# Two-layer diffusion backbone: the low parts of the first layer's up weights made by accumulating DMAs, where VectorE subtracted

## The chip, the cores and the metric

One core of one Trainium2 chip runs the whole program. The metric is device microseconds of one execution. The kernel before took 2854.1 us (median of 3 runs, 2854.01 to 2860.25). The engines are called as in the profile: PE is TensorE (PEld its weight loads), DVE is VectorE, ACT is ScalarE, POOL is GpSimd, SP is SyncE, which issues all DMAs of the kernel before.

## The reference

One inference step through two trunk layers, for 128 context tokens and 512 latent tokens of width 1024, all in float32. A layer is: modulated RMS norm, one input projection, grouped-query attention beside a bidirectional state-space scan, a gated merge with an output projection, and a convolutional feed-forward part. Only this last part is touched:

```
h = modulate(x, sh2, sc2)                                  # RMS norm, scale and shift from w_mod
u = dw_conv(h @ w_up, ffn_conv_w, ffn_conv_b)              # w_up: 1024 x 5632, conv of width 3 over tokens
u_val, u_gate = split(u)                                   # 2816 features each
x = x + g2 * ((silu(u_gate) * u_val) @ w_down)             # w_down: 2816 x 1024
```

The modulation rows (shift, scale, gate of both norms) of a layer are SiLU(cond) @ w_mod + b_mod, for two conditions.

## The kernel before, in words

**Split products.** Weights and activations are float32, the products run on float32r operands. Every operand is split in a high part (rounded to float32r by a cast) and a low part (what the rounding left, again float32r). A product is three matrix products: high by high, high by low, low by high. So each tile of weights needs a high tile and a low tile in SBUF. `wprep` (line 468) makes them: `wraw` loads a raw tile of 128 x 2048 float32, 1 MB, by one DMA on SP; ScalarE casts it into the high tile; VectorE subtracts the high tile from the raw tile into the low tile. The raw tiles (tag wr) have 2 buffers, the high tiles (wh) 3, the low tiles (wl) 3, used in turn by all weights of the kernel.

**Order of the feed-forward part.** The 22 blocks of 128 features (NFF) are taken in three groups, of 8, 8 and 6 blocks. A group is a run of up items (4, 4 and 3 of them) and then two down items. An up item (`up_item`) takes two blocks j and j + 1 of the value half and the same two of the gate half: two weight tiles of 1024 x 256, one of each half. It runs eight half products (`feat_half`): for each block, the value tile's and then the gate tile's, each over 386 and then 256 token columns, with 24 matrix products to a half (8 row blocks of the weights by three). In the first item of the layer the halves come in another order: all four of 386 columns first, then the four of 256. ScalarE takes each half out of PSUM twice (once scaled by the middle tap with the bias, once plain) into buffers whose two edge columns POOL has set to zero, VectorE adds the two other taps, ScalarE and VectorE make the SiLU product, and a split writes the result. In each half product the third matrix product is the first that reads the low tile: the order is high by high, high by low, low by high for each row block.

**Order of weights.** The main loop takes the items in order. Before it records an item it prepares weights up to two tiles beyond what the item itself needs (AHEAD = 2). With three buffers a tile's high and low buffers are those of the tile three places before.

**Beside the first layer's feed-forward part** the modulation rows of the second layer are computed (`mod_item`, class m, the lowest rank on VectorE and ScalarE): VectorE multiplies 8 pieces of w_mod of 256 KB, each by the two conditions, and accumulates them; four short products on TensorE with `pick` sum over the partitions.

**Order on the engines.** All operations are recorded first (class `Flow`), with a cost for each (`_cost`), and a planner (`issue`) simulates the engines' queues in order of time: an operation is placed when its inputs are ready and its buffers free, by rank of class and then order of record. The instructions are issued in the order of planned start times, so each engine's queue is in order, and a waiting instruction holds up what stands behind it. In `_cost` an operation on POOL counts 160 ns, or more for a power. All instructions of the kernel have line 178, that of `record`, so the profile is read by engine, operation and tile.

The lines the change touches: `_cost` (line 183 on), `wprep` (468), a new function `wsum` behind it, and the loop over up items (1491 to 1497).

Of the kernel before, what the change touches and what calls it, by code (L numbers as in the profile page):

```python
# [7 lines left out]
F32 = mybir.dt.float32  # L8
F32R = mybir.dt.float32r
# [3 lines left out]
ALU = mybir.AluOpType  # L13
# [5 lines left out]
P = 128  # L19
# [13 lines left out]
NFF = 22  # L33
# [46 lines left out]
class Flow:  # L80
# [99 lines left out]
    @staticmethod  # L180
    def _cost(lane, fn, outs, ins, kw):
        def free(ap):
            n = 1
            for d in ap.shape[1:]:
                n *= d
            return n

        n = free(outs[0])
        if lane == "dma":
            return free(outs[0]) * outs[0].shape[0] * 4 / 360.0  # L190
        if lane == "pe":
            if fn == "transpose":
                return 110.0
            if ins[0].dtype == F32R:
                return max(n, 256) / 2.4 + 2 if n > 128 else 213.0
            return max(4 * n / 2.4, 213.0)
        psum = any(a.space == PSUM for a in ins)
        scalars = sum(isinstance(a, bass.AP) for k, a in kw.items() if k in ("scale", "bias", "accum_out"))
        if lane == "act":
            return (52 if psum else 95) + 0.832 * n + 93 * scalars  # L200
        if lane == "pool":
            return 165.0 * n + 300 if ALU.pow in kw.values() else 160.0
        scalars = len(ins) - (2 if fn in ("scalar_tensor_tensor", "tensor_tensor") else 1)
        if fn == "tensor_reduce":
            return 70 + 1.04 * free(ins[0])
        if fn == "reciprocal":
            return 70 + 6.2 * n
        if fn in ("tensor_scalar", "tensor_copy", "memset"):
            return 66 + (1.04 if psum else 0.53) * n + 60 * scalars
        if fn == "scalar_tensor_tensor":  # L210
            return 70 + 1.04 * n + 60 * scalars
        return 70 + 1.04 * n
# [129 lines left out]
def hybrid_step_kernel(  # L342
# [5 lines left out]
    flow = Flow(nc)  # L348
    act, dve, pe, pool, dma = flow.act, flow.dve, flow.pe, flow.pool, flow.dma

    kp = ctx.enter_context(tc.tile_pool(name="kp", bufs=1))
    wp = ctx.enter_context(tc.tile_pool(name="wp", bufs=3))
# [11 lines left out]
    def nm(s):  # L364
        uid[0] += 1
        return f"{s}_{uid[0]}"
# [4 lines left out]
    def slabd(shape, dt=F32):  # L371
        return flow.tile(slabs, shape, dt, "slabd", nm("slab"), NSLABD)
# [5 lines left out]
    def t2(shape=(P, 512), dt=F32):  # L378
        return cv(shape, dt)
# [79 lines left out]
    def wraw(parts, wide):  # L459
        r = slabd([P, 2048]) if wide else flow.tile(wp, [P, 2048], F32, "wr", nm("wr"), 2)  # L460
        o = 0
        for ap in parts:
            a, b = ap.shape[1], ap.shape[2]
            dma.dma_start(r[:, o:o + a * b].rearrange("p (a b) -> p a b", a=a), ap)
            o += a * b
        return r, o

    def wprep(parts, wide=False):
        parts, scales = parts if isinstance(parts, tuple) else (parts, None)
        r, n = wraw(parts, wide) if wide != 2 else (None, 2048)  # L470
        hi = flow.tile(wp, [P, 2048], F32R, "wh", nm("wh"), 3)
        lo = flow.tile(wp, [P, 2048], F32R, "wl", nm("wl"), 3)
        if wide == 2:
            for j in range(4):
                o = slice(j * 512, j * 512 + 512)
                flow.cls = "d"
                t = t2()
                flow.cls = "f"
                dma.dma_start(t, parts[0][:, j, :])
                act.copy(hi[:, o], t)  # L480
                dve.tensor_sub(lo[:, o], t, hi[:, o].bitcast(F32))
        elif scales is None:
            act.copy(hi[:, 0:n], r[:, 0:n])
            dve.tensor_sub(lo[:, 0:n], r[:, 0:n], hi[:, 0:n].bitcast(F32))
        else:
            for j, w in enumerate(scales()):
                o = slice(j * 512, j * 512 + 512)
                act.mul(hi[:, o], r[:, o], w)
                dve.scalar_tensor_tensor(lo[:, o], r[:, o], w, hi[:, o].bitcast(F32), ALU.mult, ALU.subtract)
        return hi, lo  # L490

    def w_feat(w, l, c0, n=256, k0=0, kn=8):
        return [w[l, k0 * P:(k0 + kn) * P, c0:c0 + n].rearrange("(k p) f -> p k f", p=P)]
# [4 lines left out]
    def split(hi, lo, src):  # L498
        act.copy(hi, src)
        dve.tensor_sub(lo, src, hi.bitcast(F32))  # L500
# [47 lines left out]
    def feat_half(unit, cw, o, hT, b):  # L548
        ps = psf()[:, 0:HALF[b]]
        uh, ul = unit  # L550
        for kt in range(8):
            wh = uh[:, kt * cw + o:kt * cw + o + P]
            wl = ul[:, kt * cw + o:kt * cw + o + P]
            xh, xl = hT[0][b][:, kt, :], hT[1][b][:, kt, :]
            mm(ps, wh, xh, kt == 0, False)
            mm(ps, wh, xl, False, False)
            mm(ps, wl, xh, False, kt == 7)
        return ps
# [146 lines left out]
    def conv_bufs():  # L705
        raw, cc = cv()[:, 0:COLS + 2], cv()[:, 0:COLS]
        pool.memset(raw[:, 0:1], 0.0)
        pool.memset(raw[:, COLS + 1:COLS + 2], 0.0)
        return raw, cc

    def conv_in(raw, cc, ps, h, w1, b):
        o = HOFF[h]
        act.activation(cc[:, o:o + HALF[h]], ps, AF.Identity, scale=w1, bias=b)
        act.copy(raw[:, 1 + o:1 + o + HALF[h]], ps)

    def conv_taps(raw, cc, w0, w2):
        dve.scalar_tensor_tensor(cc, raw[:, 0:COLS], w0, cc, ALU.mult, ALU.add)
        dve.scalar_tensor_tensor(cc, raw[:, 2:2 + COLS], w2, cc, ALU.mult, ALU.add)

    def silu2(raw, cc):  # L720
        raw = raw[:, 0:COLS]
        act.activation(raw, cc, AF.Tanh)
        dve.scalar_tensor_tensor(cc, raw, 1.0, cc, ALU.add, ALU.mult)
# [19 lines left out]
    def add(specs, fn):  # L743
        items.append((specs, fn))
# [55 lines left out]
    def layer(l):  # L800
# [529 lines left out]
        def up_item(p, jl):  # L1330
            j0 = 8 * p + jl

            def fn(ws):
                if jl == 0:
                    nq = 2 if 8 * p + 4 < NFF else 1
                    S["g", p] = [[slabd([P, 4, PADW], F32R) for _ in range(nq)] for _ in range(2)]
                gs = S["g", p]
                f = S["fw"]
                bufs = {}

                def half(a, s, h):
                    j = j0 + a
                    if h == 0:
                        bufs[a, s] = conv_bufs()
                    raw, cc = bufs[a, s]
                    ps = feat_half(ws[s], 256, a * P, S["h2"], h)
                    conv_in(raw, cc, ps, h, f[:, 1, s, j:j + 1], f[:, 3, s, j:j + 1])
                    if h == 1:
                        conv_taps(raw, cc, f[:, 0, s, j:j + 1], f[:, 2, s, j:j + 1])
                    if h == 1 and s == 1:  # L1350
                        k = jl + a
                        cu = bufs[a, 0][1]
                        silu2(raw, cc)
                        dve.tensor_mul(cc, cc, cu)
                        split(gs[0][k // 4][:, k % 4, 0:COLS], gs[1][k // 4][:, k % 4, 0:COLS], cc)

                if p == 0 and jl == 0:
                    seq = [(a, s, h) for h in range(2) for a in range(2) for s in range(2)]
                else:
                    seq = [(a, s, h) for a in range(2) for s in range(2) for h in range(2)]  # L1360
                for a, s, h in seq:
                    half(a, s, h)
            return fn
# [127 lines left out]
        for p in range(3):  # L1491
            nk = min(8, NFF - 8 * p)
            for jl in range(0, nk, 2):
                j = 8 * p + jl
                add([w_feat(w_up, l, P * j, 256), w_feat(w_up, l, P * (NFF + j), 256)], up_item(p, jl))
                mods_next(mi)
                mi += 1
            if p == 2:
                mods_next(mi)
                if l + 1 < DEPTH:  # L1500
                    add([], lambda _: (small_tables(l + 1, Ss[l + 1]), rope_tables(l + 1, Ss[l + 1])))
            for n in range(2):
                specs = [w_tok(w_down, l, 512 * n, 8 * p + k, min(4, nk - k)) for k in range(0, nk, 4)]
                add(specs, down_item(p, n))
                if p < 2:
                    mods_next(mi)
                    mi += 1
# [4 lines left out]
    for l in range(DEPTH):  # L1512
        layer(l)
# [71 lines left out]
```

## Time and profile before

| what | before |
|---|---|
| median of 3 runs | 2854.1 us |
| the profiled execution's own time | 2856.14 us |
| its span | 2854.3 us |
| granted TensorE clock | 0.998 of full speed |
| TensorE busy | 2816.9 us, 99% |
| VectorE busy | 2067.6 us, 72% |
| ScalarE busy | 1291.3 us, 45% |
| POOL busy | 90.3 us, 3% |
| moved by DMA | 478.45 MB, 168 GB/s in the mean |

The span is the time from the first to the last instruction. The first layer's feed-forward part lies between about 950 and 1420 us of the span (the first load of an up tile is issued at 924.06), the second layer's at its end. In rows that list instructions, a merged line stands for several in a row (x4), the time behind it is from the first start to the last end, and "idle before <-releaser" tells how long the engine had waited for what. In rows of windows the busy columns are PE, PEld, DVE, ACT and POOL, in this order. A matrix product's duration in the profile is longer than the distance to the next one, since they are pipelined.

### The profile page before, as it was taken

Reading aid. Unit: us, or ns where it says so; the run is one execution under the profiler, and the core shown is the slowest. Engines: PE = TensorE matmul, PEld = TensorE weight load, DVE = VectorE, ACT = ScalarE, POOL = GpSimd, SP = SyncE. Lnnn points to the kernel's source line nnn. Section 1 sums busy time; section 2 is a strip of 40 time slices with the busy share of each in tenths; the row PEclk is TensorE's granted clock in tenths of the full one; section 3 lists DMA queues with packets and bytes.
Section 4 is the critical chain, followed back from the end, with each engine's and each line's share of the span. In section 5 each row is a group of like instructions: output and inputs, shape, how many; then the busy total and the mean of one; then the engine's idle time right before and its main releaser. Section 6 shows DMA issues by size and latency. Waiting matters only on the chain.

```text
span 2854.3 us, 41196 instructions
## 1 busy us (share of the span) xinstructions
PE 2816.9 (99%) x15620; PEld 2455.4 (86%) x15620; DVE 2067.6 (72%) x2851; ACT 1291.3 (45%) x2255; POOL 90.3 (3%) x408
## 2 busy tenths in 40 slices
PE   7999999999999999999999999999999999999999
PEld 4898997788788898998979989878887888989898
DVE  7878775987799599997677666598778456545554
ACT  6454544445353453442444645544454325524342
POOL 1100000000000000000011000000000000000000
PEclk9999999999999999999999999999999999999999
DMA  7344344676768546455352323457667654251523
GB/s 260 104 126 137 114 151 155 209 255 245 276 214 277 177 139 213 164 180 174 104 164 83 95 94 100 151 203 251 221 241 250 205 171 136 86 166 65 157 83 111
DMA packets 309679, 478.45 MB, mean 168 GB/s; under 512 B 19808, under 2 KB 139792, under 8 KB 304360
## 3 DMA queue, kind: packets, MB, share of 16 engines
q1 hardware_dynamic: 309480, 475.81, 49.8%
q8 instruction: 123, 2.02, 0.3%
q14 instruction: 76, 0.62, 0.1%
HBM read 384.08 MB, written 91.65 MB: 167 GB/s over the span
## 4 chain that ended last, share of the span: by engine, by line
PE 94%; DMA 3%; DVE 1%; ACT 1%; issue 0%; SPq 0%; DVEq 0%; ACTq 0%
PE pf L178 79%; PE p L178 10%; PE pp L178 3%; PE pq L178 1%; DMA slab<-in_w_mod_dram 0%; DVE tmp L178 0%; DVE wl L178 0%; DMA tmp<-in_state_ssd_dram 0%; DMA tmp<-sz 0%; DMA mw<-in_w_mod_dram 0%; DMA tmp<-in_x_prompt_dram 0%; DVE slab L178 0%; DMA tmp<-xs 0%; ACT tmp L178 0%; DMA slab<-row 0%
## 5 line engine op out<-in xcount | busy, mean ns | idle before, releaser
L178 PE MATMUL pf<-wh,slab 128*128 128x512 f32 x3920 | 1268.9, 400 | 6.5 <-DVE tmp L178 2.5
L178 PE MATMUL pf<-slab,wh 128*128 128x256 f32 (+1 forms) x4416 | 979.5, 311 | 3.3 <-DVE slab L178 1.9
L178 PEld LDWEIGHTS pf<-wh,slab 128*128 128x128 f32 x3920 | 733.3, 189 | 175.8 <-issue 7.6
L178 PE MATMUL pf<-wl,slab 128*128 128x512 f32 x1960 | 781.5, 399 | 0.2 <-DVE wl L178 0.2
L178 PEld LDWEIGHTS pf<-slab,wh 128*128 128x128 f32 x4416 | 741.1, 188 | 11.9 <-issue 5.5
L178 PE MATMUL pf<-slab,wl 128*128 128x256 f32 (+1 forms) x2208 | 684.5, 310 | 0.0
L178 DVE TENSOR_TENSOR wl<-wr,wh 128x2048 fp32r<-128x2048 f32 (+1 forms) x156 | 350.7, 2248 | 144.4 <-ACT wh L178 143.8
L178 PEld LDWEIGHTS pf<-wl,slab 128*128 128x128 f32 x1960 | 369.6, 189 | 87.1 <-issue 5.8
L178 ACT CAST wh<-wr 128x2048 fp32r<-128x2048 f32 (+1 forms) x156 | 293.0, 1879 | 319.9 <-PE pf L178 302.3
L178 PEld LDWEIGHTS pf<-slab,wl 128*128 128x128 f32 x2208 | 415.6, 188 | 3.1 <-issue 0.2
L178 DVE SCALAR_TENSOR_TENSOR tmp<-tmp,fw,tmp 128x642 f32<-128x642 f32 x176 | 155.5, 885 | 81.0 <-ACT tmp L178 67.0
L178 PE MATMUL p<-tmp,slab 128*128 128x64 f32 (+1 forms) x976 | 209.9, 336 | 1.4 <-DMA tmp<-xs 1.0
L178 ACT ACTIVATE tmp<-tmp 128x642 f32<-128x642 f32 (+2 forms) x176 | 120.9, 687 | 180.1 <-DVE tmp L178 142.3
L178 ACT ACTIVATE tmp<-pf,fw 128x386 f32<-128x386 f32 (+1 forms) x176 | 108.9, 619 | 175.9 <-PE pf L178 172.6
L178 DVE TENSOR_TENSOR tmp<-pf,tmp 128x512 f32<-128x512 f32 x100 | 68.3, 688 | 133.9 <-PE pf L178 133.4
L178 PEld LDWEIGHTS p<-tmp,slab 128*128 128x128 f32 x976 | 136.2, 190 | 17.3 <-ACT tmp L178 4.4
L178 ACT COPY tmp<-pf 128x256 f32<-128x256 f32 (+3 forms) x296 | 127.3, 431 | 43.9 <-PE pf L178 43.8
L178 DVE TENSOR_TENSOR slab<-tmp,slab 128x512 fp32r<-128x512 f32 (+4 forms) x182 | 109.0, 634 | 41.5 <-ACT slab L178 41.3
L178 DVE SCALAR_TENSOR_TENSOR macc<-tmp,cT,macc 128x512 f32<-128x512 f32 x196 | 137.8, 743 | 0.8 <-DMA tmp<-in_w_mod_dram 0.8
L178 DVE TENSOR_TENSOR tmp<-tmp,tmp 128x512 f32<-128x512 f32 (+3 forms) x190 | 133.6, 705 | 5.7 <-DMA tmp<-sz 3.0
L178 ACT ACTIVATE tmp<-pf 128x512 f32<-128x512 f32 (+1 forms) x110 | 63.5, 577 | 141.5 <-PE pf L178 133.6
L178 PEld LDWEIGHTS p<-cst,tmp 128*128 128x128 f32 (+2 forms) x750 | 91.7, 140 | 39.4 <-issue 13.1
(131 smaller groups left out, 2622.1 us busy)
## 6 DMA issues: line engine op xcount, KB each, us to landing
wr<-in_w_in_dram SPq DMA_DIRECT2D x60, 1024.0 KB
wr<-in_w_up_dram SPq DMA_DIRECT2D x44, 1024.0 KB
slab<-row SPq DMA_DIRECT2D x40, 1024.0 KB
tmp<-in_w_mod_dram SPq DMA_DIRECT2D x116, 256.0 KB
tmp<-xres SPq DMA_DIRECT2D x85, 256.0 KB
wr<-in_w_down_dram SPq DMA_DIRECT2D x20, 1024.0 KB
tmp<-xs SPq DMA_DIRECT2D x72, 256.0 KB
xres<-tmp SPq DMA_DIRECT2D x70, 256.0 KB
```

Source lines behind the costliest of these rows:

```text
L178: self.ops.append((lane, lambda: call(*args, **kw), self._cost(lane, fn, outs, ins, kw), deps, touched, self.cls))
```

## The change

For the first layer's up weights the low tile is made in another way. ScalarE casts the raw tile into the high tile as before, and then writes the negated high tile into the low tile. POOL issues a DMA that reads the same weights from HBM once more and adds them to what stands in the low tile. VectorE does nothing for these tiles. The low tile then holds weights minus high part, as before. It is done for all 22 tiles (11 items by two) of the first layer; all other weights are as before. In the planner a DMA issued on POOL counts 5000 ns of POOL's time.

```diff
@@ _cost
         if lane == "act":
             return (52 if psum else 95) + 0.832 * n + 93 * scalars
+        if fn == "dma_start":
+            return 5000.0
@@ wprep
     def wprep(parts, wide=False):
+        if callable(parts):
+            return parts()
...
+    def wsum(parts):
+
+        r, n = wraw(parts, False)
+        hi = flow.tile(wp, [P, 2048], F32R, "wh", nm("wh"), 3)
+        lo = flow.tile(wp, [P, 2048], F32R, "wl", nm("wl"), 3)
+        act.copy(hi[:, 0:n], r[:, 0:n])
+        act.mul(lo[:, 0:n], hi[:, 0:n].bitcast(F32), -1.0)
+        o = 0
+        for ap in parts:
+            a, b = ap.shape[1], ap.shape[2]
+            pool.dma_start(
+                lo[:, o:o + a * b].rearrange("p (a b) -> p a b", a=a), ap.bitcast(F32R), accum_op=ALU.add
+            )
+            o += a * b
+        return hi, lo
@@ layer
-                add([w_feat(w_up, l, P * j, 256), w_feat(w_up, l, P * (NFF + j), 256)], up_item(p, jl))
+                us = [w_feat(w_up, l, P * j, 256), w_feat(w_up, l, P * (NFF + j), 256)]
+                if l == 0:
+                    us = [lambda u=u: wsum(u) for u in us]
+                add(us, up_item(p, jl))
```

## Rows read from the trace of the kernel before

**Rows 1.** The page, part 1: busy us of each engine (share of the span) xinstructions.

```profile
PE 2816.9 (99%) x15620; PEld 2455.4 (86%) x15620; DVE 2067.6 (72%) x2851; ACT 1291.3 (45%) x2255; POOL 90.3 (3%) x408
```

**Rows 2.** Windows: stretch, length, busy us (xinstructions) by engine, clock, DMA share, GB/s.

```profile
1000.00:1100.00 100.00, 100.00 (x698) 98.16 (x697) 94.36 (x119) 52.55 (x84) 1.73 (x24) 1.00 0.46 148
1044.90:1073.80 28.90, 28.90 (x198) 28.36 (x197) 27.46 (x36) 15.07 (x24) 0.71 (x8) 1.00 0.45 147
1420.00:2854.32 1434.32, 1423.16 (x7883) 1248.82 (x7882) 926.72 (x1247) 628.67 (x1098) 42.67 (x200) 1.00 0.46 152
2400.00:2450.00 50.00, 50.00 (x356) 50.00 (x355) 29.91 (x30) 25.18 (x41) 1.01 (x16) 1.00 0.19 64
```

**Rows 3.** TensorE's waits, 924 to 1420 us: us in total, times, longest.

```profile
PE pf L178 <- DVE slab L178: 1.0, 1, 1.0
PE pf L178 <- ACT slab L178: 0.7, 1, 0.7
```

**Rows 4.** ScalarE in order of time: start, us, instruction [idle before <-releaser].

```profile
1033.87 1.91 ACT L178 CAST wh<-wr 128x2048 fp32r<-128x2048 f32 x1 [1.58 <-PE pf L178]
1035.68 0.72 ACT L178 CAST slab<-tmp 128x642 fp32r<-128x642 f32 x1
...
1062.80 1.92 ACT L178 CAST wh<-wr 128x2048 fp32r<-128x2048 f32 x1 [0.58 <-PE pf L178]
...
2437.88 1.91 ACT L178 CAST wh<-wr 128x2048 fp32r<-128x2048 f32 x1 [0.74 <-PE pf L178]
...
2465.83 1.91 ACT L178 CAST wh<-wr 128x2048 fp32r<-128x2048 f32 x1 [0.73 <-PE pf L178]
```

**Rows 5.** TensorE's groups in one up item, 1033.8 to 1062.7 us.

```profile
L178 PE MATMUL p<-tmp,pick 128*2 128x512 f32 x4 | 1.6, 396 | 0.0
```

**Rows 6.** VectorE's and ScalarE's groups, 944 to 1365 us: busy, mean ns | idle before.

```profile
L178 DVE TENSOR_TENSOR wl<-wr,wh 128x2048 fp32r<-128x2048 f32 x30 | 68.7, 2290 | 15.2 <-ACT wh L178 15.2
...
L178 DVE TENSOR_SCALAR macc<-tmp,cT 128x512 f32<-128x512 f32 x24 | 10.6, 474 | 0.0
...
L178 ACT CAST wh<-wr 128x2048 fp32r<-128x2048 f32 x30 | 57.4, 1914 | 109.7 <-PE pf L178 96.3 <-DMA tmp<-xres 12.6 <-ACT tmp L178 0.8
```

**Rows 7.** Waits of SP's queue, 945 to 1420 us.

```profile
SPq L178 <- DVE wl L178: 222.7, 33, 20.5
```

**Rows 8.** POOL in order of time, one pair of memsets.

```profile
1041.22 0.13 POOL L178 MEMSET tmp<- 128x1 f32 x2 [7.48 <-DVE tmp L178]
```

**Rows 9.** TensorE in order of time: first product with a gate tile's low part.

```profile
986.10 0.34 PE L178 MATMUL pf<-slab,wl 128*128 128x386 f32 x1
...
1019.46 0.34 PE L178 MATMUL pf<-slab,wl 128*128 128x386 f32 x1
...
1048.11 0.34 PE L178 MATMUL pf<-slab,wl 128*128 128x386 f32 x1
...
1164.56 0.34 PE L178 MATMUL pf<-slab,wl 128*128 128x386 f32 x1
...
1337.44 0.34 PE L178 MATMUL pf<-slab,wl 128*128 128x386 f32 x1
```

**Rows 10.** ScalarE in order of time: casts of the four tight gate tiles.

```profile
974.03 1.91 ACT L178 CAST wh<-wr 128x2048 fp32r<-128x2048 f32 x1 [1.63 <-PE pf L178]
...
1009.16 1.92 ACT L178 CAST wh<-wr 128x2048 fp32r<-128x2048 f32 x1 [1.20 <-PE pf L178]
...
1153.44 1.92 ACT L178 CAST wh<-wr 128x2048 fp32r<-128x2048 f32 x1 [14.28 <-PE pf L178]
...
1326.34 1.91 ACT L178 CAST wh<-wr 128x2048 fp32r<-128x2048 f32 x1 [23.51 <-PE pf L178]
```

**Rows 11.** SP's issue of an up load; windows of the DMA engines (columns as rows 2).

```profile
1038.13 0.38 SPq L178 DMA_DIRECT2D wr<-in_w_up_dram  x1
...
1039.00:1042.50 3.50, 3.50 (x28) 3.50 (x27) 3.43 (x5) 2.01 (x2) 0.13 (x2) 1.00 0.89 298
1046.00:1046.50 0.50, 0.50 (x6) 0.50 (x6) 0.50 (x2) 0.28 (x1) 0.00 (x0) 1.00 0.95 70
```

## The prediction

> **What bounds the kernel now.** I read the page's busy times first [rows 1]: TensorE is busy in 2816.9 of 2854.3 us, VectorE in 72%, ScalarE in 45%, GpSimd in 3%. TensorE leaves 37 us idle in the whole span, so no other engine's time is worth more than that. Then the stretches by stage [rows 2]: in the up stage of the first layer (1000 to 1100 us) TensorE is busy all the time while VectorE is at 94%. So VectorE looks crowded exactly where the change works. The test of whether that costs anything is the waits of TensorE over the stage, 924 to 1420 us: 1.0 and 0.7 us, and none on a low part [rows 3]. A second test is the same stage of the second layer, which has the same products without the modulation sums. There one up item (two weight tiles) takes 27.95 us, from one cast at 2437.88 to the same cast of the next item at 2465.83. In the first layer it takes 28.93 us [rows 4]. The 0.98 us between them go with four products p<-tmp,pick of the modulation, the only group that the first layer's item has beyond the tile products [rows 5]. So a VectorE at 94% costs TensorE nothing, and what the change takes from it can give back at most the 1.7 us of waits.
>
> **What the change does, part by part.**
>
> *VectorE.* 22 subtractions of 2.29 us [rows 6] go: 50 us of VectorE, 4.6 of its 27.5 us in an item [rows 2]. Worth at most 1.7 us on the path (above), and at least nothing. I take 0.
>
> *ScalarE.* 22 negations of 128x2048 from SBUF to SBUF come. The nearest row is the cast of the same size, 1.91 us [rows 6]: 42 us in all, 3.8 in an item, where ScalarE is busy for 15.1 of 28.9 us [rows 2]. So it is hidden in throughput, but it stands in the chain of every tile. If its cover were gone it would cost up to these 42 us.
>
> *SP's queue.* A raw tile comes free after the cast, no longer after the subtraction, so its next load is issued some 2 us earlier. SP waits for subtractions during 222.7 us of 945 to 1420 [rows 7], but no cast waits for a weight load: 96.3 of the 109.7 us that ScalarE idles before casts end on TensorE, which frees the buffer of the high part, and 12.6 on a store of the residual [rows 6]. Worth 0; the loads only move closer to the new transfers.
>
> *POOL's queue.* It gets 22 issues, each waiting for a negation. Behind them stand the small memsets at the edges of the convolution buffers (0.13 us for a pair, here 7.48 us after the one before) [rows 8]. The taps on VectorE need those. The planner charges 5 us on POOL for an issue, so it spreads the memsets around it. Cost 0, unless writing an issue takes POOL much more than these 5 us; no row of before shows an issue on POOL.
>
> *DMA engines.* 22 accumulating transfers of 1 MB come, beside the loads that stay. This is the term that decides.
>
> **The chain of a tile.** An item uses a value tile and a gate tile; call the gate tile B. It is the second in use, and its high and low buffers (three of each) come free at three quarters of the item before, when that item's value tile is done. For the B in [rows 4] the cast starts at 1033.87, and its first product with a low part starts at 1048.11 [rows 9]: 14.2 us. Now: cast 1.91, subtraction 2.29, and ten microseconds to spare. Then: cast 1.91, one instruction of ScalarE that gets in between, 0.7 (the next one after this cast starts at 1035.68 and lasts 0.72) [rows 4], negation 1.91, together 4.5; so 9.7 us are left from the issue on POOL to the landing. Seven of the eleven B tiles are like this. Four have less: the first two of the stage (another order of halves in the first item) and the first after each down stage. Their casts start at 974.03, 1009.16, 1153.44 and 1326.34, their first low products at 986.10, 1019.46, 1164.56 and 1337.44 [rows 9, 10]. Less 4.5 each, 7.6, 5.8, 6.6 and 6.6 us are left, 26.6 in sum. The value tiles have a whole item, 28.9 us, and don't wait. With L for the time from issue to landing, TensorE stalls for 7 x (L - 9.7) + (4L - 26.6), each bracket and each of the four terms from zero up.
>
> **L from both sides.** A plain load of an up tile is issued at 1038.13; its bytes run from 1039.0 to 1042.5, at a mean of 298 GB/s, which is the tile's 1.05 MB [rows 11]: 0.9 + 3.5 = 4.4 us. That is the low end, and with it the sum is 0. For the high end, the slowest busy stretch near it is that of 1046.0 to 1046.5, where the engines are at 0.95 and move 70 GB/s [rows 11]; the tile at that rate takes 15.0, so L = 15.9 and the sum is 7 x 6.2 + 37.0 = 80 us. I take a value nearer to the load, since source rows, sizes and destination are the load's: an accumulation has to read its destination as well as its source, so the engines read 2 MB where the load reads 1 (3.5 us more, L = 7.9). Loads of raw tiles run in the same engines in the same stretch, moved toward it by SP's earlier issue; a transfer that shares them with one load ends up to 3.5 us later (L = 11.4). The two transfers take 14 us of engine time in an item of 28.9 us whose share is 0.45 already [rows 2], which makes 0.93: there will be sharing in nearly every item. Sum: 7 x 1.7 + (45.6 - 26.6) = 11.9 + 19.0 = 31 us.
>
> Two pages of the Trainium skill bear on L and disagree. "DMA: Bandwidth & Descriptors" (Anatomy of one DMA, the GpSimd path) fits 2.0 us plus bytes at 436 GB/s: by it 1 MB takes an estimated 4.4 us, as the load in the trace does, and the sum would be 0. "Collectives: The Full Stack" (Part 3, the bandwidth ceiling) says that a reducing transfer needs two source reads per chunk and runs at half a copy's rate; by it the data part is 7.0 us and the sum, with sharing, that 31. No run here shows an accumulating transfer yet.
>
> The profiled execution took 2856.14 us with a span of 2854.3, the median of the runs is 2854.1. The stall is added to either: 2887 for a profiled execution, **2885 us** for the median.
>
> **Rivals.**
>
> 1. *Not slower: the transfer is hidden.* Place: the gate tiles' landing on TensorE. If the accumulation moves as fast as a load or shares little, L is 4.4 to 8.8, and the sum 0 to 4 x 8.8 - 26.6 = 8.6 us, less the waits of at most 1.7: 2852 to 2863, likeliest 2854. For it: the engines are at 0.46 in the stage [rows 2], and a load alone takes 4.4. Against it: the second read. It decides at L = 8.8, where the four tight tiles alone make 0.3%.
> 2. *Bound by rate.* If POOL takes long to issue a tile of 1024 rows, or the addition itself is slow, L is 15 or more: 80 us at the high end above, 2934. If two transfers of 15 us then fill the engines beside the 13 us that an item's loads take (0.45 of 28.9), an item lasts 43 us, 11 x 14 = 154 us more: 3008. For it: no row shows an issue on POOL or an addition in a DMA. Against it: the loads with the same rows move at 298 GB/s [rows 11].
> 3. *Faster by the freed VectorE.* The modulation sums run earlier, the waits of 1.0 and 0.7 us vanish, and the planner's new order may close others. It needs 8.6 us to be told from nothing, out of some 13 us that TensorE idles after 924 us (1.7 in the stage, 11.2 after 1420) [rows 2, 3]; against it stands the second layer's stage, where VectorE is at 30 of 50 us [rows 2] and TensorE gains nothing. 2841 at best.
>
> "SBUF — State Buffer" (Who interferes with whom) in the Trainium skill adds a lock: GpSimd can't write descriptors while VectorE runs an instruction in a two-port mode, as a tensor_scalar may. No trace here shows such a conflict; the only long group of that kind in the stage has 474 ns each [rows 6], so by that rule 11 gate tiles would lose an estimated 0.5 us each, 5.5 in all, inside the range.
>
> **Chances.** Forecast (L from 8.8 to 13.5, a sum of 9 to 54 us, 2863 to 2908): 0.40. Hidden: 0.28. Bound by rate: 0.27. Faster by VectorE: 0.05. Less than 0.3%, 8.6 us, can't be told from no change here. So slower is 0.40 and 0.27, 0.67; the same 0.28; faster 0.05. The range for 8 in 10 runs from 2852, the hidden case with the waits gone, to 2950, past the 80 us but short of full engines.
>
> **What would show it.** Right: TensorE waits for a DMA into wl, once per up item, 1 to 3 us in the seven plain items and 4 to 6 at the four tight ones; VectorE 50 us shorter, ScalarE 42 us longer; the DMA share of the up stage near 0.9; nothing changed after 1420 us but the shift. A landing under 8.8 us after POOL's issue would make it wrong to the fast side; more than 14, or memsets on POOL that come late for the taps, to the slow side.

## The result, and the profile after

The changed kernel takes 2901.35 us (median of 4 runs, 2897.46 to 2904.81) where the kernel before takes 2854.06 us on the same chip (4 runs): a ratio of 1.0155 [1.0139, 1.017], 47.3 us slower, 16 us beyond the 2885 us forecast. The profiled execution took 2897.46 us with a span of 2895.7, 41.4 us more than the 2854.3 of before; the other 6 us are the spread of the runs (this execution lies 3.9 us below its median, that of before 2.1 us above). The working below is for the 41.4 us.

First the page's busy times:

```profile
PE 2826.6 (98%) x15620; PEld 2462.0 (85%) x15620; DVE 2020.2 (70%) x2829; ACT 1327.9 (46%) x2277; POOL 120.7 (4%) x430
```

Against [rows 1], VectorE lost 47.4 us and ScalarE gained 36.6, close to what 22 subtractions and 22 negations make. TensorE is the line to stop at: the same 15620 products are busy for 9.7 us longer. So the 41.4 us are two things, some 31 us of idle time and some 10 us of slower products.

TensorE's waits from 924 to 1460 us, the stretch that answers to [rows 3] (us in total, times, longest):

```profile
PE pf L178 <- DMA wl<-in_w_up_dram: 26.7, 6, 6.5
PE p L178 <- ACT tmp L178: 4.4, 5, 1.9
PE p L178 <- DVE tmp L178: 0.9, 2, 0.6
PE pf L178 <- ACT slab L178: 0.7, 1, 0.7
```

Before it was 1.7 us. The long wait is the accumulation into the low tile. Of the two lines on `p`, the 4.4 us behind ScalarE are modulation products (`p<-tmp,pick`, [rows 5]), which waited for nothing before; the 0.9 us behind VectorE are two groups of products of the norm (`p<-cst,tmp`, at 962.08 and 966.13). In order of time, the six waits for accumulations:

```profile
993.65 0.66 PE L178 MATMUL pf<-slab,wl 128*128 128x386 f32 x1 [5.93 <-DMA wl<-in_w_up_dram]
...
1033.68 0.66 PE L178 MATMUL pf<-slab,wl 128*128 128x386 f32 x1 [6.21 <-DMA wl<-in_w_up_dram]
...
1188.35 0.69 PE L178 MATMUL pf<-slab,wl 128*128 128x386 f32 x1 [6.40 <-DMA wl<-in_w_up_dram]
...
1251.40 0.45 PE L178 MATMUL pf<-slab,wl 128*128 128x386 f32 x1 [1.21 <-DMA wl<-in_w_up_dram]
...
1375.87 0.69 PE L178 MATMUL pf<-slab,wl 128*128 128x386 f32 x1 [6.50 <-DMA wl<-in_w_up_dram]
...
1406.99 0.44 PE L178 MATMUL pf<-slab,wl 128*128 128x386 f32 x1 [0.49 <-DMA wl<-in_w_up_dram]
```

The four of about 6 us are the four tight gate tiles of [rows 9, 10], 25.0 us together; the plain gate tiles make 1.7.

The issues on POOL, the columns as for instructions, the last line for all 22 (us):

```profile
L178 POOL DMA_DIRECT2D wl<-in_w_up_dram x22: 1540/1549/1730, 950.2 to 1425.6; - x22
...
DMA to landing us min/median/max: 9.0/12.1/19.1
```

The forecast's L was 11.4; the median is 12.1, and POOL writes an issue in 1.5 us, of the 5 us for which the planner charges it. The median mixes three kinds of tile, though: taken one by one, the seven plain gate tiles landed after 9.0 to 10.8 us (9.8 in the mean), the four tight ones after 11.6, 10.1, 12.7 and 12.7, and the eleven value tiles, which have a whole item of time, after 10.1 to 19.1 (16.1 in the median). The DMA queues from 924 to 1460 us (packets, MB, share of 16 engines):

```profile
q1 hardware_dynamic: 54236, 80.09, 45.5%
q0 software_dynamic: 22880, 23.07, 27.8%
```

The second queue is POOL's. 27.8% of 536 us over 22 tiles is 6.8 us of all 16 engines for each accumulated MB; the forecast had 7.0. This is the time of the packets, and packets overlap (the windows below have shares of 1.2), so part of it can be time spent waiting for other packets.

Now the slower products. Windows after the four stalls (columns as in [rows 2]):

```profile
994.00:998.00 4.00, 4.00 (x14) 4.00 (x14) 0.00 (x0) 0.00 (x0) 0.00 (x0) 0.50 1.24 198
998.00:1000.00 2.00, 2.00 (x10) 2.00 (x9) 0.00 (x0) 0.00 (x0) 0.00 (x0) 0.76 0.55 87
...
1034.00:1036.00 2.00, 2.00 (x7) 2.00 (x7) 0.56 (x1) 0.00 (x0) 0.00 (x0) 0.50 1.17 264
...
1186.00:1188.00 2.00, 0.00 (x0) 0.00 (x0) 0.00 (x0) 0.00 (x0) 0.00 (x0) 0.67 1.18 242
1188.00:1192.00 4.00, 3.65 (x11) 3.65 (x12) 1.47 (x2) 0.00 (x0) 0.11 (x2) 0.50 1.17 261
1192.00:1194.00 2.00, 2.00 (x9) 2.00 (x9) 0.88 (x2) 0.00 (x0) 0.02 (x1) 0.62 1.15 274
...
1376.00:1380.00 4.00, 4.00 (x13) 4.00 (x14) 1.47 (x2) 0.00 (x0) 0.13 (x2) 0.50 1.23 213
```

The granted clock falls while TensorE stands idle for some 6 us, and is still at its lower level (0.50, 1.2 of 2.4 GHz) when the products go on at full busy share. The products themselves show where it rises again, here after the last of the four:

```profile
1378.92 0.53 PE L178 MATMUL pf<-slab,wl 128*128 128x386 f32 x1
1379.89 0.52 PE L178 MATMUL pf<-slab,wl 128*128 128x386 f32 x1
...
1381.58 0.34 PE L178 MATMUL pf<-slab,wl 128*128 128x386 f32 x1
1382.11 0.34 PE L178 MATMUL pf<-slab,wl 128*128 128x386 f32 x1
```

Three products of 386 columns take 0.97 us at first and 0.53 us later. Read like this, the half level covers 5.3, 2.7, 5.1 and 5.3 us of work after the four stalls, 18.4 us, of which by those two times 45% is lost: 8.3 us.

The other windows set the account (same columns; the first line is the stage before the change):

```profile
924.00:1420.00 496.00, 494.34 (x2938) 452.96 (x2938) 400.21 (x522) 208.16 (x331) 12.96 (x105) 1.00 0.49 163
...
1050.00:1100.00 50.00, 50.00 (x339) 48.86 (x338) 44.72 (x63) 31.50 (x45) 5.72 (x17) 1.00 0.87 222
...
924.00:1460.00 536.00, 502.80 (x2926) 458.20 (x2925) 351.04 (x497) 244.84 (x353) 44.92 (x127) 0.97 0.74 193
1460.00:2895.70 1435.70, 1424.84 (x7892) 1250.62 (x7890) 927.67 (x1250) 628.54 (x1098) 41.61 (x200) 1.00 0.46 152
```

TensorE idles 33.2 us from 924 to 1460, against 1.7 in the stretch of before; after it 10.9, against 11.2 [rows 2]. In the stage it is busy for 8.5 us longer, which the 8.3 us of half clock explain. So 31.5 us of idle time and 8.5 of slower products make 40.0 of the 41.4 us, in the stage of the change.

### The profile page after: what moved, and what is told of

The parts are those of the page before. It is cut to its first block, busy times and chain, and to the rows that moved or that the text cites. A ratio compares the mean times of both kernels' runs of the same rounds, so it can differ in the third digit from the quotient of the medians.

```text
span 2895.7 us, 41244 instructions
## 1 busy us (share of the span) xinstructions
PE 2826.6 (98%) x15620; PEld 2462.0 (85%) x15620; DVE 2020.2 (70%) x2829; ACT 1327.9 (46%) x2277; POOL 120.7 (4%) x430
## 4 chain that ended last, share of the span: by engine, by line
PE 86%; DMA 7%; issue 3%; DVE 3%; ACT 1%; SPq 0%; POOL 0%; DVEq 0%; ACTq 0%; POOLq 0%
PE pf L178 71%; PE p L178 9%; PE pp L178 3%; DMA wl<-in_w_up_dram 2%; PE pq L178 1%; DVE tmp L178 1%; DMA tmp<-in_state_ssd_dram 1%; ACT tmp L178 1%; DMA tmp<-in_w_mod_dram 1%; DVE macc L178 1%; DVE slab L178 1%; DMA ga<-tmp 1%; DMA xres<-tmp 1%; DMA slab<-in_w_mod_dram 0%; SPq L178 0%
## 5 line engine op out<-in xcount | busy, mean ns | idle before, releaser
L178 PE MATMUL pf<-slab,wl 128*128 128x256 f32 (+1 forms) x2208 | 689.5, 312 | 26.8 <-DMA wl<-in_w_up_dram 26.7
L178 DVE TENSOR_TENSOR wl<-wr,wh 128x2048 fp32r<-128x2048 f32 (+1 forms) x134 | 300.3, 2241 | 136.3 <-ACT wh L178 135.8
L178 PEld LDWEIGHTS p<-tmp,slab 128*128 128x128 f32 x976 | 136.1, 190 | 16.1 <-ACT tmp L178 4.4
L178 DVE TENSOR_TENSOR tmp<-tmp,tmp 128x512 f32<-128x512 f32 (+3 forms) x190 | 133.7, 705 | 11.8 <-DMA tmp<-xres 7.4
L178 PEld LDWEIGHTS p<-cst,tmp 128*128 128x128 f32 (+2 forms) x750 | 91.2, 140 | 42.7 <-issue 14.3
## 6 DMA issues: line engine op xcount, KB each, us to landing
wl<-in_w_up_dram POOLq DMA_DIRECT2D x22, 1024.0 KB, 12.1
```

The lines of the kernel that those rows point to most:

```text
L178: self.ops.append((lane, lambda: call(*args, **kw), self._cost(lane, fn, outs, ins, kw), deps, touched, self.cls))
```

## The experiments

All stand against the kernel before on the same chip. "PE busy" is the page's busy time of TensorE (2816.9 before, 2826.6 after), "landing" the least and the median time from POOL's issue to landing.

| kernel | median us | ratio to before | PE busy | landing |
|---|---|---|---|---|
| e1 tight tiles back on VectorE | 2872.31 | 1.0048 [1.0033, 1.0063] | 2822.2 | 8.9 / 12.3 |
| e2 only the tight tiles | 2884.72 | 1.009 [1.0075, 1.0105] | 2826.6 | 9.5 / 10.6 |
| e3 copied, not added | 2873.27 | 1.0049 [1.0031, 1.0067] | 2822.7 | 5.5 / 7.8 |
| e4 added by VectorE | 2854.75 | 0.9993 [0.9984, 1.0002] | 2811.9 | |
| e5 added from the raw tile | 2884.64 | 1.0106 [1.0091, 1.0121] | 2822.2 | 6.8 / 7.7 |
| e6 second layer instead | 2896.55 | 1.0147 [1.013, 1.0164] | 2829.3 | 9.0 / 11.4 |
| e7 gate tile later | 2893.75 | 1.0132 [1.0116, 1.0147] | 2826.7 | 9.0 / 13.9 |
| e8 second layer, tight back | 2859.12 | 1.002 [1.001, 1.0029] | 2817.5 | 8.9 / 10.9 |
| e9 second layer, gate later | 2868.28 | 1.0054 [1.0038, 1.007] | 2819.5 | 8.9 / 11.2 |
| e10 gate later, no accumulation | 2857.49 | 1.0013 [1.0004, 1.0022] | 2815.5 | |
| e11 e7, costs in the planner | 2873.41 | 1.0072 [1.0056, 1.0087] | 2820.8 | 9.2 / 13.1 |

None beats the kernel before; e4 equals it.

### e1 and e2: the four tight tiles, and the others

```diff
@@ e1 (e2 has the two branches the other way round)
-                    us = [lambda u=u: wsum(u) for u in us]
+                    us = [u if n == 1 and 4 * p + jl // 2 in (0, 1, 4, 8) else (lambda u=u: wsum(u)) for n, u in enumerate(us)]
```

> The four tight gate tiles (the first two of the stage and the first after each down stage) are made by VectorE's subtraction again, the other 18 by accumulating DMAs. Theory 1 (the change costs what TensorE stalls at the landing of the four tight tiles, 5.9 to 6.5 us each, and the half clock after each, some 2 us): 25 + 8 us of the 47 go and the plain gate tiles' 2 us stay, so 2856 to 2864. Theory 2 (the accumulations load the DMA engines and slow the stage as a whole): 18 of 22 transfers keep 18/22 of the loss, about 2892. Theory 3 (the planner's new order and ScalarE's longer chain): most of the loss stays, over 2880.

> The converse: only the four tight gate tiles are made by accumulating DMAs. Theory 1: four stalls of 4 to 6.5 us and the half clock after each, so 20 to 36 us over before, 2874 to 2890. Theory 2: 4 of 22 transfers, 9 us, 2863. Theory 3: less than 10 us over before.

The two parts add up: by the ratios, of 2854 us, e1 loses 13.7 and e2 25.7, together 39.4 where the whole change loses 44.2; by the medians, against 2855.93 for the kernel before on their chip, it is 16.4 and 28.8, together 45.2 of 47.3. In e2 TensorE waits for accumulations 4 times, 21.2 us in all, where 19.0 were forecast for the four. e1 was expected below 2864 and missed that; its waits, 924 to 1460 us:

```profile
PE p L178 <- ACT tmp L178: 6.5, 4, 2.2
PE pf L178 <- DMA wl<-in_w_up_dram: 2.7, 3, 1.1
PE p L178 <- DVE tmp L178: 1.7, 3, 0.6
```

With the tight tiles gone the low parts cost 2.7 us, far from the 11.9 that the forecast had for seven plain tiles. The modulation products cost 7.0 of the 8.2 us on `p` (1.2 are the norm's), a wait that the forecast didn't have.

### e3 and e5: what makes the transfer long

```diff
@@ e3: the addition is left out (the low tile then holds the raw weights)
-            pool.dma_start(
-                lo[:, o:o + a * b].rearrange("p (a b) -> p a b", a=a), ap.bitcast(F32R), accum_op=ALU.add
-            )
+            pool.dma_start(lo[:, o:o + a * b].rearrange("p (a b) -> p a b", a=a), ap.bitcast(F32R))
@@ e5: one accumulation from the raw tile in SBUF, in place of the loop
-        for ap in parts:
...
+        pool.dma_start(lo[:, 0:n], r[:, 0:n].bitcast(F32R), accum_op=ALU.add)
```

> All 22 transfers are issued on POOL after the negation as in the change, but copy plainly instead of adding (the low tiles then hold the weights themselves, so the output is not the reference's). If the second read of an accumulation makes the landing late (12.1 us in the median after the change), a plain copy lands in 5 to 8.5 us, the tight tiles stall 0 to 2 us each and the time is 2854 to 2864. If POOL's issue (1.55 us) or the queue it goes through is what is slow, or the share with the loads alone, it lands in 10 us or more and the time stays over 2885.

> The accumulating DMA adds the raw tile that is in SBUF already, 128 rows of 8 KB, where the change reads the weights from HBM again in 1024 rows of 1 KB. If the bytes of two reads and one write set the landing, it stays at 10 to 12.5 us and the time at 2885 to 2905. If the short rows or HBM do, it lands in 6 to 8.5 us, and the time is 2854 to 2866. Raw tiles then stay taken until the landing, so SP's loads are issued later than in the change.

Without the addition the same rows from HBM land 3.5 us sooner at the least (5.5 against 9.0) and 4.3 in the median, and the POOL queue's share, of 526 us, falls:

```profile
q0 software_dynamic: 22880, 23.07, 17.1%
```

That is 4.1 us of all engines for a tile against 6.8 with the addition. So the addition costs 2.7 us of every engine and the 3.5 us of landing that the forecast took for a second read of 1 MB; that it is a read isn't shown. The time came to 2873, not the 2854 to 2864 expected: three of the tight tiles still stall, for 2.3, 4.1 and 4.1 us, where their copies landed after 6.2, 10.8 and 10.4 us. The profile puts the first of these, at 1021.98, down to ScalarE, but the product came 0.1 us after the landing.

From SBUF with rows of 8 KB the accumulation lands after 7.7 us in the median, and takes 5.4 us of the engines (22.4% of 526 us). Source and length of rows changed together here, so which of them shortens it stays open. But the time stayed at 2884.64. TensorE's waits there:

```profile
PE p L178 <- ACT tmp L178: 8.1, 4, 3.2
PE pf L178 <- DMA wl<-wr: 7.8, 5, 2.9
PE p L178 <- DVE tmp L178: 6.2, 3, 4.9
```

The waits on low parts fell from 26.7 to 7.8 us, and those on `p` rose from 5.3 to 14.3; the longest of these, 4.9 us, is a product of the norm (at 971.69). A raw tile is now held until its accumulation has read it, and with two of them the next loads come later; that this is what delays the products on `p` was argued, not shown, so on time e5 tells nothing of the change itself.

The Trainium skill's "DMA: Bandwidth & Descriptors" (Anatomy of one DMA, the GpSimd path), by which the forecast noted an estimated 4.4 us, is not borne out beside these loads: 9.0 us at the least for an accumulation, and 5.5 for the plain copy. "Collectives: The Full Stack" (Part 3, the bandwidth ceiling), two source reads and half a copy's rate, is stated for a ReduceScatter and stands nearer: the copy (e3) and the accumulation take 4.1 and 6.8 us of the engines, 1.7 times and not twice.

### e4: the same chain and order without the DMA

```diff
-        for ap in parts:
...
+        dve.tensor_add(lo[:, 0:n], r[:, 0:n], lo[:, 0:n].bitcast(F32))
```

> ScalarE negates as in the change, and VectorE adds the raw tile where POOL issued the DMA: everything of the change but the transfers. Theory 1 and 2: no loss, 2852 to 2860, since TensorE waits for the transfers. Theory 3 (ScalarE's 1.92 us in the chain of each tile and in the norm's stage): 2865 or more.

ScalarE negates as in the change, and an addition stands where the subtraction stood: 0.9993 [0.9984, 1.0002]. So the negations, with the longer chain on ScalarE, cost nothing by themselves; all of the loss comes with the DMA: its transfer, its issue on POOL, or the plan made around it.

### e6 and e8: the second layer, which has no modulation beside

```diff
-                if l == 0:
+                if l == 1:
@@ e8 has e1's choice of tiles as well
```

> The second layer's up tiles are made by accumulating DMAs, the first layer's by VectorE. There are no modulation loads beside that stage (DMA share 0.2 to 0.3 before) and VectorE is at 60%. Theory 1 with the share of modulation loads in the landing: it lands in 9 to 10.5 us, stalls of 2.5 to 5 us at the four tight tiles, none at the plain ones, 12 to 30 us over before: 2866 to 2884. If the accumulation alone is that slow whatever runs beside it: as the change, 2890 to 2905. If VectorE's load had a part in it (a crowded VectorE that gains from the change), the second layer would lose more than the first.

> In the second layer, where no modulation is computed beside the up stage, 18 tiles are made by accumulating DMAs and the four tight gate tiles by VectorE. In the first layer this left 16 us. If those 16 us came by the modulation (its loads share the DMA engines, and TensorE waits in order for its products with pick), nothing of them is here: 0 to 5 us over before, 2854 to 2859, from the plain gate tiles alone. If 18 accumulations cost that much by themselves (plain gate tiles, the residual loads of the down stage), 2866 to 2872 again.

e6's only long wait, 2380 to 2850 us:

```profile
PE pf L178 <- DMA wl<-in_w_up_dram: 29.5, 6, 7.6
```

There is no wait on `p`, and VectorE had 40% of its time free in this stage before [rows 2]; the loss is 42.0 us (0.0147 of 2854) all the same. With the tight tiles back on VectorE (e8) 18 accumulations cost 5.7 us by the ratio, and PE busy is that of before. TensorE waits for them once, 2380 to 2870 us:

```profile
PE pf L178 <- DMA wl<-in_w_up_dram: 1.6, 1, 1.6
```

Against e1's 13.7 us this says that some 8 us of what e1 lost come with the modulation beside it; of e8's own 5.7, what lies beyond the wait isn't explained.

### e7, e9, e10 and e11: the gate tile used later

```diff
@@ up_item (e7, e9, e10): both blocks of the value tile first
-                    seq = [(a, s, h) for h in range(2) for a in range(2) for s in range(2)]
+                    seq = [(a, s, h) for h in range(2) for s in range(2) for a in range(2)]
...
-                    seq = [(a, s, h) for a in range(2) for s in range(2) for h in range(2)]
+                    seq = [(a, s, h) for s in range(2) for a in range(2) for h in range(2)]
@@ the planner (e11): POOL 1.55 us, DMA engines 6.8 us, landing 9 us or later
+                if e == "pool" and cost == 5000.0:
+                    free[e] = tb + 1550.0
+                    xfer = max(xfer, tb + 2000.0) + 6800.0
+                    end = max(tb + 9000.0, xfer)
```

e9 is this order with the accumulation in the second layer only, e10 with none.

> The change with another order in the up items of both layers: both blocks of the value tile first, then both of the gate tile. A gate tile then has 10 us or more from issue to first use everywhere, the plain ones a whole item. Theory 1: nearly no stall, no low clock, 2854 to 2864, with all 22 transfers in place. Theory 2 (load on the DMA engines): the loss stays, over 2885.

> The control of the other order: the kernel before, without any accumulating DMA, with the value tile's blocks first in every up item. TensorE had no stall there to win back or to lose: 2850 to 2860. If it is slower than 2865, the order itself costs, and the runs with it are to be read against this one.

> In the second layer all 22 tiles are made by accumulating DMAs, and the up items of both layers take the value tile's two blocks before the gate tile's. If the landing at the tight gate tiles and the modulation are all there is, only the first gate tile stalls, some 4.5 us, and the clock after it: 2856 to 2864. If late gate tiles were not the cause, it stays near the 2896 of the second layer with the old order.

> The change in the first layer with the value tile's blocks first, and a planner that counts an accumulation as 1.55 us on POOL, 6.8 us of the DMA engines and 9 us at least to the landing (in the change: 5 us on POOL and no transfer). The kernel with that order but the old plan lost 40 us, 22 of them in waits of TensorE for modulation products. If the plan put these products ahead of loads that it believed to be free, they move back: 2855 to 2870. If the load on the DMA engines holds up the residual and modulation loads whatever the plan, 2880 or more.

The order alone costs 3 to 4 us (e10). In the second layer it does what it should: 28 us come back between e6 and e9 by the medians, 26.5 by the ratios, the waits for low parts fall from 29.5 to 8.8 us and PE busy from 2829.3 to 2819.5. One wait of 5.35 us at the first gate tile remains, and two below 2 us; 2868.28 is 4 us over the 2856 to 2864 expected. In the first layer it brought back 8 us and no more. e7's waits, 924 to 1460 us:

```profile
PE p L178 <- DVE tmp L178: 14.0, 4, 6.6
PE p L178 <- ACT tmp L178: 8.3, 2, 7.9
PE pf L178 <- DMA wl<-in_w_up_dram: 5.2, 2, 4.5
```

The low parts fell from 26.7 to 5.2 us, and the modulation products took their place, with 21.2 us (the other 1.0 on `p` is the norm's). The longest DVE wait can be followed in order of time over all engines:

```profile
1140.16 1.01 SPq L178 DMA_DIRECT2D wr<-in_w_up_dram  x2
...
1142.44 1.56 POOL L178 DMA_DIRECT2D wl<-in_w_up_dram  x1 [53.66 <-ACT wl L178]
1145.09 0.55 SPq L178 DMA_DIRECT2D tmp<-xres  x1
...
1158.36 0.69 DVE L178 TENSOR_TENSOR tmp<-tmp,tmp 128x512 f32<-128x512 f32 x1 [7.43 <-DMA tmp<-xres]
...
1159.71 0.59 PE L178 MATMUL p<-tmp,pick 128*2 128x512 f32 x1 [6.63 <-DVE tmp L178]
```

A load of 256 KB of the residual is issued behind two up loads and an accumulation. It is on the chain of waits for 13.15 us before VectorE's addition can start; the split of the modulation sum stands behind that addition in VectorE's queue, and the product with `pick` in TensorE's queue behind that. The two other long waits lead back to loads of 256 KB as well: that of 7.85 us (at 1208.27) to a piece of w_mod, issued at 1179.96 and 17.10 us on the chain, that of 6.28 us (at 1351.96) to a load of the residual, issued at 1337.98 and 12.51 us on it.

Told the measured costs, the planner (e11) places these otherwise: the products with `pick` wait no longer and those with low parts for 1.1 us in all, 20 us come back by the medians (17 by the ratios), and most of the rest sits in one new wait, in the norm stage:

```profile
991.23 1.97 PE L178 MATMUL p<-cst,tmp 128*128 128x128 f32 x8 [10.63 <-DVE tmp L178]
```

2873.41 is a little over the 2855 to 2870 expected. The chain that ends in this product, in order of time (start, us, what):

```profile
979.22 5.69 DMA tmp<-xres
...
985.72 1.81 ACT wl L178
...
987.81 1.55 POOL wl L178
989.36 0.23 POOL sm L178
...
990.68 0.50 DVE tmp L178
```

After a load of the residual, the negation on ScalarE and the issue on POOL stand in front of the norm's small operations on POOL, 3.4 us together: two engines that the forecast costed at 0. Whether these costs in the planner help in the old order of halves isn't shown by any run.

## Why the prediction was right, and where its sum was off

*The mechanism and the sign.* TensorE waits for the landing at the four tight gate tiles, as the forecast had it (e1, e2). "Hidden" needed L of at most 8.8; the least measured is 9.0. "Bound by rate" needed 15 or a POOL that issues slowly; an issue takes 1.5 us, and only value tiles, which no product waited for, landed after 15 us or more. "Faster by the freed VectorE": 47.4 us of VectorE went, and no run that frees it (e1 to e3, e5 to e9, e11) is faster; the bound of 1.7 us [rows 3] was the right reading of an engine that is 94% busy. The forecast's terms for the DMA engines hold: 7.0 us of engine time against 6.8, a DMA share of 0.93 against 0.87 in an undisturbed stretch (1050 to 1100 us). ScalarE's negations were rightly costed at 0 where the plan has them (e4); in e11's plan one of them and an issue on POOL are on the path.

*The tight tiles: 19.0 forecast, 25.0 measured.* The step that was short is "4.5 us from the cast to the issue". The first tight tile on ScalarE:

```profile
974.21 1.91 ACT L178 CAST wh<-wr 128x2048 fp32r<-128x2048 f32 x1 [1.36 <-PE pf L178]
976.02 1.49 ACT L178 ACTIVATE tmp<-p,sm 128x128 f32<-128x128 f32 x4
977.39 0.64 ACT L178 ACTIVATE tmp<-tmp 128x512 f32<-128x512 f32 x1
...
979.66 1.92 ACT L178 ACTIVATE wl<-wh 128x2048 fp32r<-128x2048 f32 x1
```

POOL's issue follows at 981.88: 7.7 us from the cast's start, because 3.5 us of norm work got between, where one instruction of 0.7 was taken. The trace of before has the same norm work behind the same cast, so this could have been read ahead:

```profile
975.84 1.50 ACT L178 ACTIVATE tmp<-p,sm 128x128 f32<-128x128 f32 x4
...
978.86 0.64 ACT L178 ACTIVATE tmp<-tmp 128x512 f32<-128x512 f32 x1
```

For the four tiles it is 7.7, 6.1, 6.4 and 7.0 us, 9.1 more than 4 x 4.5. From issue to the product they took 11.8, 10.3, 12.7 and 12.8 us, 1.9 more than 4 x 11.4. TensorE's need came 4.9 us later than the before's rows said, 49.5 us after the casts in all against 44.6. 19.0 + 9.1 + 1.9 - 4.9 is the 25.1.

*The plain tiles: 11.9 forecast, 1.7 measured.* One L, 11.4, was used for every tile. The plain gate tiles landed after 9.8 us in the mean, next to the 9.7 that were left; the two that waited had 10.8 (issue at 1240.51) and 10.0 us (at 1396.90), and the other five didn't wait. The 3.5 us for sharing with a load, right at the tight tiles, were too much here. With a bracket of (L - 9.7) counted seven times, a microsecond of L is 7 us of sum; this was the term to give a range of its own.

*Two terms that were missing.* The half clock after each long stall, 8.3 us: the sum took a stall for its length alone. And the waits on `p`, 5.3 us here, of which the modulation products make 4.4, with 7.0 in e1 and 21.2 in e7. The forecast asked what the busy DMA engines do to the accumulation, not what the accumulation does to the small loads of others. Such loads stood in its own rows: the 12.6 us that it read as a store of the residual end on a load (`tmp<-xres`, [rows 6]). e6 and e8, where there is no modulation, have no waits of modulation products. That these waits lead back to late loads is shown for the three long ones of e7 (above). For the changed kernel's own five it isn't: VectorE waits there for loads of 4 KB (b_mod) during 25.5 us, 8 times, and in the kernel before not at all, but behind the product at 1241.65 the chain runs over ScalarE's cast and negation of a weight tile (1235.04 and 1238.23) and over no load.

Together 6.0 more on the tight tiles, 8.3 and 5.3 for the missing terms, and 10.2 less on the plain tiles: 9.4 of the 10 us by which the profiled span grew beyond 31. That the forecast came within 16 us is in part luck, since the plain tiles' surplus stood in for terms that it didn't have.

The lock of the Trainium skill's "SBUF — State Buffer" (Who interferes with whom), weighed in the forecast, doesn't show: POOL's issues take 1540 to 1730 ns all through the stage. Which of VectorE's instructions overlapped an issue isn't shown, so this refutes nothing.

*What stays open.* The split of e5's loss, and what makes the changed kernel's own modulation products late. The PE busy of e1 and e3, 5 us above before, is in large part half clock too: e1 has a stretch of 3.4 us at 0.50 in the stage, behind two waits of 1.3 and 0.5 us (at 1190.5), e3 has 9.3 us of work at 0.50 behind its two long stalls, and both have two more such stretches after 2100 us. Before has one at 1440 and two before 70 us, e4 (2811.9) none of these three: outside the long stalls they come and go between executions.

## What to carry to other kernels

An engine that is 94% busy but makes nobody wait gives back nothing, and a DMA that takes over its work pays in landing time at the tiles with the least slack: list the slack of every tile, and count from the issue, with whatever the queue of the engine before it lets in between. Ask of a new stream of transfers also which small loads it will stand in front of, and tell the planner what it costs. Read the landing of the tiles that somebody waits for, not the median of all. Count a TensorE stall of several microseconds at more than its length, since here each of 6 us was followed by 3 to 5 us of work at half the clock.

## What the runs showed of the hardware

- An accumulating DMA of 1 MB from HBM in rows of 1 KB, issued on POOL, lands after 9.0 us at the least (median 12.1) and its packets take 6.8 us of all 16 DMA engines; the same rows copied 5.5 (7.8) and 4.1; accumulated from SBUF in rows of 8 KB 6.8 (7.7) and 5.4. All of this is beside other loads.
- POOL is taken for 1.55 us by the issue of an accumulation of 1024 rows, 0.87 by that of a copy of them, 0.86 by that of 128 long rows accumulated.
- In idle stretches of 5.9 to 6.5 us the granted clock of TensorE fell to 1.2 GHz, and it rose after 2.7 to 5.3 us of work. In e6, with waits up to 7.6 us, PE busy is 12.4 us above before.
